# A graph attention kernel: one-hots split around the weights, gathers in two passes, keys in halves, and integer keys

## The chip, the cores and the metric

One core of a Trainium2 chip runs the whole kernel. The metric is the time of one execution on the device in microseconds (us). The profile is of one execution; its span, from first to last instruction, is some 2 us shorter than the time measured from outside, so I compare spans with spans and times with times. For one core, a run counts as fast when it is within 1.5% of the fastest of its kernel.

## The reference

```python
# x [4096, 64], edge_index [2, 50000], weight [4, 64, 64], att_src/att_dst [4, 64]
for h in range(4):
    x_proj[h] = x @ weight[h]
    edge_scores[h] = (x_proj[h, src] * att_src[h]).sum(-1) + (x_proj[h, dst] * att_dst[h]).sum(-1)
edge_scores = np.where(edge_scores > 0, edge_scores, 0.2 * edge_scores)
# output[h, dst] += exp(score) * x_proj[h, src], over all edges
# output[h, dst] /= (sum of exp(score) over the edges of dst) + 1e-8
return output.transpose(1, 0, 2).reshape(4096, 256)
```

## The kernel before

The 50,000 edges are sorted on VectorE in two passes, through memory, into 33 blocks of 125 destination nodes. Each block has 16 groups (one for each segment of 256 source nodes) of 128 edge slots. A window of sorted keys is unpacked into two small indices per slot (`tb`), written to a table in memory (`gat_bins`), and each block loads its piece of it, repeated over all partitions (`bc`). Block 0 does not go through memory: TensorE spreads `tb` over the partitions (`spread`).

In the loop, one-hot matrices (`oh`, an equality against the partition number) let TensorE gather each edge's features and attention terms into PSUM (`ps`). ScalarE takes the exponentials (`ex`) and copies the gathered rows (`xs`); VectorE makes the weights (`wv`, the larger of two exponentials) and the weighted features (`val`). Matmuls sum them per destination (`acc`), ScalarE copies the sums (`aT`), TensorE projects them (`pf`), and each second block VectorE divides (`inv`, `res`) and stores two blocks.

```python
class Windows:                                   # hand-over: keys -> indices
    def unpack(self, i, *engs):
        V.tensor_scalar(out=self.kb[:, i, :], in0=self.win[:, i, :], scalar1=boff[:, i:i + 1], scalar2=None, op0=OP.add)
        V.tensor_scalar(out=self.t[:, i, 0, :], in0=self.kb[:, i, :], scalar1=8, ..., op0=OP.logical_shift_right)
        V.tensor_scalar(out=self.t[:, i, 1, :], in0=self.kb[:, i, :], scalar1=SG - 1, ..., op0=OP.bitwise_and)
        V.tensor_copy(out=self.tb[:, i], in_=self.t[:, i])
        for k, eng in enumerate(engs):
            eng.dma_start(out=<bin_dram piece k of group i>, in_=self.tb[:, i, k, :])

CH = ((0, 6), (6, 6), (12, 4))                   # the 16 segments in three chunks
class Blocks:
    def gather(self, b, c, copy=S.copy):
        ...                                      # ps: two buffers
        for i in range(n):
            T.matmul(out=ps[:, i, P:P + XC], lhsT=oh[:, 1, e], rhs=xa[:, 2 * t, :], ...)
            T.matmul(out=ps[:, i, P:P + XC], lhsT=oh[:, 2, e], rhs=xa[:, 2 * t + 1, :], ...)
            T.matmul(out=ps[:, i, 0:S0], lhsT=oh[:, 0, e], rhs=adb[:, b, :], ...)
        S.activation(out=<ex>, in_=<ps>, func=ACTF.Exp)
        copy(out=xs[:, t0:t0 + n, 0:P + XC], in_=ps[:, 0:n, 0:P + XC])

    def run(self, also={}):
        for c in range(len(CH)):
            self.gather(0, c, V.tensor_copy if c == 1 else S.copy)
        self.onehot(1)                           # both halves: oh[:, 0:2], then oh[:, 2]
        for b in range(ND):
            self.load(b + 4)
            self.weigh(b, ...)                   # wv = max(ex0, ex1); val = xs * wv
            self.gather(b + 1, 0)
            self.onehot(b + 2)
            if b:
                self.sink.project(b - 1)
                if b % 2 == 0:
                    self.sink.give(b - 2, 2)     # inv, res, output
            self.sums(b, -1)                     # opens with a matmul on a vector of ones
            self.gather(b + 1, 1)
            self.gather(b + 1, 2)
            self.sums(b, 0)                      # the value matmuls
            self.sums(b, 1)
        ...

class Finish:                                    # pf: one buffer, of two blocks
    def project(self, b):
        for k in range(2):
            T.matmul(out=self.pf[0:BD, b % 2, k * P:(k + 1) * P], lhsT=self.aT[:, b % 2, k * BD:(k + 1) * BD], rhs=Wbd[:, k, :], ...)   # fp32, BD = 125
    def give(self, b, n):
        V.reciprocal(out=inv[0:BD, 0:n], ...)
        V.tensor_tensor(out=res[0:BD, 0:n], in0=<pf>, in1=<inv>, op=OP.mult)
        ...
```

## Time and profile before

| | before |
|---|---|
| time, median of 4 runs beside the changed kernel | 302.66 us (301.87 to 302.71) |
| span of the profiled run, mean granted clock | 300.1 us, 0.854 |
| busy: VectorE, PE, weight loads, ScalarE | 88%, 68%, 64%, 60% of the span |
| first operation of the first / second sort | 7.64 / 76.68 us |
| window of sorted keys in place | 120.14 us |
| first `val` | 133.29 us |
| `val` of block 3 to `val` of block 31 | 135.81 us |
| last `res` | 293.51 us |

The shares are averages over stages with different limits. The rows of times are what to read: keys and two sorts (VectorE alone), a hand-over between the window's arrival and the first `val`, and a steady loop of 33 blocks. The stretches and timelines that carry this are shown in the prediction.

### The profile page before, as it was taken

How to read it: one execution, taken by the hardware profiler on the slowest of the kernel's cores; microseconds unless marked ns; L12 is line 12 of the kernel's file. 1: busy time of each engine (PE TensorE's matmuls, PEld its weight loads, DVE VectorE, ACT ScalarE, POOL GpSimd, SP SyncE). 2: the span in 40 equal slices, each digit the busy share in tenths (PEclk: the TensorE clock that was granted, in tenths of full speed). 3: DMA queues.
4: the chain of work that ended last, by engine and by line, in shares of the span. 5: the costliest groups of instructions: out<-in, count | busy, mean ns of one | idle time of the engine just before them, and what ended most of it. 6: DMA issues, size and time to landing. Idle time of an engine off the chain costs nothing. (4 is left out here: it accounts for less than half of the span.)

```text
span 300.1 us, 8417 instructions
## 1 busy us (share of the span) xinstructions
PE 203.3 (68%) x3534; PEld 191.8 (64%) x3534; DVE 265.2 (88%) x493; ACT 180.4 (60%) x353; POOL 27.6 (9%) x77
## 2 busy tenths in 40 slices
PE   0001899950000003759999999999999999999980
PEld 0000599950000000449999999999999999999980
DVE  4999999994799995799999999999999999999970
ACT  2950710050699910347887778778777878787740
POOL 7982000002000002300000000000000000000000
PEclk9999975555555555798999999999999999999998
DMA  3025000001000001497486667865686667755012
GB/s 107 0 55 105 0 2 0 0 0 54 19 0 0 0 0 44 149 356 269 157 303 249 201 221 288 279 224 193 259 303 224 210 227 306 273 177 210 11 38 58
DMA packets 13070, 41.80 MB, mean 139 GB/s; under 512 B 3088, under 2 KB 8272, under 8 KB 8928
## 3 DMA queue, kind: packets, MB, share of 16 engines
q1 hardware_dynamic: 10632, 38.97, 36.5%
q10 hardware_dynamic: 1688, 1.55, 2.1%
q0 software_dynamic: 704, 0.66, 1.0%
q8 instruction: 30, 0.49, 0.7%
q14 instruction: 16, 0.13, 0.1%
HBM read 36.13 MB, written 5.05 MB: 137 GB/s over the span
## 5 line engine op out<-in xcount | busy, mean ns | idle before, releaser
L467 ACT CAST xs<-ps 128x1200 bf16<-128x1200 f32 (+1 forms) x98 | 102.7, 1048 | 0.0
L480 DVE TENSOR_TENSOR val<-xs,wv 128x4096 bf16<-128x4096 bf16 (+1 forms) x34 | 75.7, 2229 | 4.8 <-ACT xs L467 1.3
L459 PE MATMUL ps<-xa,oh 128*128 128x72 bf16 x528 | 72.3, 197 | 3.6 <-DVE oh L441 2.9
L463 PE MATMUL ps<-adb,oh 128*128 128x136 bf16 x528 | 73.2, 226 | 0.0
L461 PE MATMUL ps<-xa,oh 128*128 128x72 bf16 x528 | 71.5, 198 | 0.6 <-DVE oh L442 0.5
L499 PE MATMUL acc<-xs,val 128*128 128x125 bf16 x1056 | 64.0, 219 | 1.1
L499 PEld LDWEIGHTS <-val 128*128 128x128 bf16 x1056 | 59.4, 98 | 3.4 <-DVE val L480 3.4
L459 PEld LDWEIGHTS <-oh 128*128 128x128 bf16 x528 | 52.3, 99 | 3.5 <-DVE oh L441 3.5
L461 PEld LDWEIGHTS <-oh 128*128 128x128 bf16 x528 | 52.0, 99 | 2.0 <-DVE oh L442 1.4
L463 PEld LDWEIGHTS <-oh 128*128 128x128 bf16 x528 | 52.1, 99 | 0.0
L441 DVE TENSOR_SCALAR oh<-bc,pF 128x4096 bf16<-128x4096 bf16 (+2 forms) x35 | 42.7, 1220 | 0.6 <-ACT bc L425 0.6
L465 ACT ACTIVATE ex<-ps 128x96 bf16<-128x96 f32 (+1 forms) x99 | 25.1, 253 | 29.8 <-PE ps L463 29.8
L204 DVE TENSOR_TENSOR sA<-sB 128x256 f32<-128x256 f32 (+2 forms) x108 | 38.8, 400 | 1.9
L204 DVE TENSOR_TENSOR sB<-sA 128x256 f32<-128x256 f32 (+2 forms) x100 | 35.9, 400 | 1.7
L277 PE MATMUL cnt_ps<-sgn,sel 128*128 128x17 f32 (+1 forms) x6 | 1.7, 390 | 41.9 <-ACT sgn L269 41.9
L277 PEld LDWEIGHTS cnt_ps<-sgn,sel 128*128 128x128 f32 x6 | 1.4, 318 | 42.0 <-issue 42.0
L442 DVE TENSOR_SCALAR oh<-bc,pF 128x2048 bf16<-128x2048 bf16 (+2 forms) x35 | 25.1, 717 | 0.0
L361 PEld LDWEIGHTS at_ps<-uv,xT 64*128 64x128 f32 x130 | 24.7, 296 | 0.4 <-issue 0.4
L361 PE MATMUL at_ps<-uv,xT 64*128 64x4 f32 x130 | 24.8, 327 | 0.0
L266 ACT ACTIVATE junk<-kr,nb 128x512 f32<-128x512 f32 x33 | 23.8, 722 | 1.1
L545 PE MATMUL pf<-Wbd,aT 128*125 128x128 f32 x132 | 21.9, 288 | 0.9 <-ACT aT L541 0.9
L344 PE MATMUL ps<-ident,wS 64*128 64x64 f32 x2 | 0.7, 350 | 28.6 <-DMA wS<-in_weight_dram 28.6
(128 smaller groups left out, 222.5 us busy)
## 6 DMA issues: line engine op xcount, KB each, us to landing
bc<-gat_bins SPq DMA_DIRECT2D x32, 1024.0 KB, 8.9
out_dram<-res SPq DMA_DIRECT2D x32, 125.0 KB
gat_sorted<-sA SPq DMA_DIRECT2D x2, 256.0 KB
eS<-in_edge_index_dram SPq DMA_DIRECT2D x1, 390.0 KB
eD<-in_edge_index_dram ACTq DMA_DIRECT2D x1, 390.0 KB
gat_bins<-tb SPq DMA_DIRECT2D x9, 32.0 KB
out_dram<-res SPq DMA_DIRECT2D x1, 96.0 KB
win<-gat_sorted,wi POOLq DMA_INDIRECT x5, 2.7
```

Source lines behind the costliest of these rows:

```text
L204: V.tensor_tensor(out=av(d[:], o, [2 * h, n], [1, h]), in0=av(s[:], 0, [2 * h, n], [1, h]), in1=av(s[:], h, [2 * h, n], [1, h]), op=op)
L266: S.activation(out=junk[:], in_=v, func=ACTF.Sign, bias=nbnd[:, b:b + 1], scale=1.0, accum_out=sgn[:, b:b + 1])
L361: T.matmul(out=ps[:, b, :], lhsT=xT[:, b * step:b * step + P], rhs=uv[:, k, :], start=(b == 0), stop=True, skip_group_check=True)
L441: V.tensor_scalar(out=oh[:, 0:2, e], in0=bc[:, :, e], scalar1=pF[:, 0:1], scalar2=None, op0=OP.is_equal)
L442: V.tensor_scalar(out=oh[:, 2, e], in0=bc[:, 1, e], scalar1=pF[:, 1:2], scalar2=None, op0=OP.is_equal)
L459: T.matmul(out=ps[:, i, P:P + XC], lhsT=oh[:, 1, e], rhs=xa[:, 2 * t, :], start=(i % 2 == 0), stop=False, skip_group_check=True)
L461: T.matmul(out=ps[:, i, P:P + XC], lhsT=oh[:, 2, e], rhs=xa[:, 2 * t + 1, :], start=False, stop=False, skip_group_check=True)
L463: T.matmul(out=ps[:, i, 0:S0], lhsT=oh[:, 0, e], rhs=adb[:, b, :], start=False, stop=True, skip_group_check=True)
L465: S.activation(out=av(ex[:], 2 * t0, [2, n], [2 * NT, 2 * H], [1, 2]), in_=av(ps[:], P, [PW, n], [1, 2 * H], [0, 2]), func=ACTF.Exp)
L467: copy(out=xs[:, t0:t0 + n, 0:P + XC], in_=ps[:, 0:n, 0:P + XC])
L480: V.tensor_tensor(out=av(val[:], h * Dout, [Dout, n], [C, NT], [1, Din]), in0=av(xs[:], S0, [0, n], [XW, NT], [1, Din]), in1=av(wv[:], h * ...
L499: T.matmul(out=self.acc[:, k * BD:(k + 1) * BD], lhsT=val[:, t, k * P:(k + 1) * P], rhs=xs[:, t, 0:BD], start=False, stop=(t == NT - 1), s ...
```

## The change

Its intent: keep VectorE from waiting on its own previous result, and start each stage sooner. (1) In the loop `wv` of the next block moves between the two one-hot operations, and `inv` ahead of them, so that no operation directly follows the one whose result it reads. (2) The gather takes the matmuls that need the second one-hot half in a second pass. (3) The projection uses 128 weight columns. (4) In the hand-over: six warming matmuls for nine, a ScalarE copy in place of a VectorE one for block 0, shorter unpacking. (5) Input and first keys come in two halves. (6) The second sort's last step writes integers, which the unpacking then needs no conversion for.

```diff
+    EH = EL // 2
+    for e in (slice(0, EH), slice(EH, E0)):             # one load per tensor before
+        for t, k, eng in ((eS, 0, nc.sync), (eD, 1, nc.scalar)):
+            eng.dma_start(out=t[:, e, :], ...)
...
-        store(skey2, so.runs())
+        ki = pool.tile([P, L], I32, name="ki")
+        store(skey2, so.runs(ki))                       # skey2 is int32 now
...
         def unpack(self, i, *engs):
-            V.tensor_scalar(out=self.kb[:, i, :], in0=self.win[:, i, :], scalar1=boff[:, i:i + 1], ..., op0=OP.add)
-            ... shift, and, then V.tensor_copy(out=self.tb[:, i], in_=self.t[:, i])
+            t, tb = self.t[:, i], self.tb[:, i]
+            V.tensor_scalar(out=t[:, 1, :], in0=self.win[:, i, :], scalar1=SG - 1, ..., op0=OP.bitwise_and)
+            V.tensor_scalar(out=t[:, 0, :], in0=self.win[:, i, :], scalar1=8, ..., op0=OP.logical_shift_right)
+            (S.copy if i == 0 else V.tensor_copy)(out=tb[:, 1, :], in_=t[:, 1, :])
+            V.tensor_scalar(out=tb[:, 0, :], in0=t[:, 0, :], scalar1=boff[:, i:i + 1], ..., op0=OP.add)
...
                 T.matmul(out=ps[:, i, P:P + XC], lhsT=oh[:, 1, e], rhs=xa[:, 2 * t, :], ...)
-                T.matmul(out=ps[:, i, P:P + XC], lhsT=oh[:, 2, e], rhs=xa[:, 2 * t + 1, :], ...)
                 T.matmul(out=ps[:, i, 0:S0], lhsT=oh[:, 0, e], rhs=adb[:, b, :], ...)
+            for i in range(n):
+                T.matmul(out=ps[:, i, P:P + XC], lhsT=oh[:, 2, <e of i>], rhs=xa[:, 2 * t + 1, :], ...)
...
             for c in range(len(CH)):
-                self.gather(0, c, V.tensor_copy if c == 1 else S.copy)
+                self.gather(0, c)                       # ScalarE copies all three
             self.onehot(1)
+            self.weights(0)
             for b in range(ND):
                 self.load(b + 4)
-                self.weigh(b, ...)
+                self.values(b, ...)                     # val alone
                 self.gather(b + 1, 0)
-                self.onehot(b + 2)
                 if b:
                     self.sink.project(b - 1)
-                    if b % 2 == 0:
-                        self.sink.give(b - 2, 2)
                 self.sums(b, -1)
                 self.gather(b + 1, 1)
                 self.gather(b + 1, 2)
+                pair = b and b % 2 == 0
+                if pair:
+                    self.sink.invert(2)
+                self.onehot(b + 2, halves=(0,))
+                self.weights(b + 1)
+                self.onehot(b + 2, halves=(1,))
+                if pair:
+                    self.sink.give(b - 2, 2)            # res, output
                 self.sums(b, 0)
                 self.sums(b, 1)
...
-                T.matmul(out=self.pf[0:BD, b % 2, ...], lhsT=self.aT[:, b % 2, k * BD:(k + 1) * BD], ...)
+                T.matmul(out=self.pf[:, b % 2, ...], lhsT=self.aT[:, b % 2, k * BD:k * BD + P], ...)
...
+        for e, n in ((0, EH), (EH, EL - EH)):           # the four key operations, on one half at a time
...
-        for i in range(9):
+        for i in range(6):
             T.matmul(out=warm[:], lhsT=identb[:], rhs=adb[:, 0:4, 0:P], start=True, stop=True)
```

More of the change, by code (lines that the diff above doesn't have):

```diff
@@ L59 @@
     skey1 = nc.dram_tensor("gat_sorted1", (1, P * L + W1), F32).ap()
-    skey2 = nc.dram_tensor("gat_sorted2", (1, P * L + W2), F32).ap()
+    skey2 = nc.dram_tensor("gat_sorted2", (1, P * L + W2), I32).ap()
     bin_dram = nc.dram_tensor("gat_bins", (8 * NI, 2, NR, W2), BF16).ap()
@@ L70 @@
     eD = cst.tile([P, EL, 2], I32)
-    for t, k, eng in ((eS, 0, nc.sync), (eD, 1, nc.scalar)):
-        eng.dma_start(out=t[:, 0:E0, :], in_=ei[k, 0:P * E0, :].rearrange("(p e) c -> p e c", p=P))
+    EH = EL // 2
+    for e in (slice(0, EH), slice(EH, E0)):
+        for t, k, eng in ((eS, 0, nc.sync), (eD, 1, nc.scalar)):
+            eng.dma_start(out=t[:, e, :], in_=ei[k, 0:P * E0, :].rearrange("(p e) c -> p e c", p=P)[:, e, :])
     if rem:
@@ L141 @@
     pg = cst.tile([P, 1], F32)
-    G.tensor_scalar(out=pg[:], in0=pm16[:], scalar1=-float(SG * N), scalar2=None, op0=OP.mult)
+    G.tensor_scalar(out=pg[:], in0=pm16[:], scalar1=-float(N), scalar2=None, op0=OP.mult)
     for i in range(NI):
-        G.tensor_scalar(out=boff[:, i:i + 1], in0=p16[:], scalar1=-float(BD * SG), scalar2=-float(8 * i * BD * SG),
+        G.tensor_scalar(out=boff[:, i:i + 1], in0=p16[:], scalar1=-float(BD), scalar2=-float(8 * i * BD),
                         op0=OP.mult, op1=OP.add)
@@ L161 @@
     nc.gpsimd.dma_start(out=skey1[0:1, P * L:P * L + W1], in_=pad[:])
-    nc.gpsimd.dma_start(out=skey2[0:1, P * L:P * L + W2], in_=pad[:, 0:W2])
+    padi = cst.tile([1, W2], I32)
+    G.tensor_copy(out=padi[:], in_=pad[:, 0:W2])
+    nc.gpsimd.dma_start(out=skey2[0:1, P * L:P * L + W2], in_=padi[:])
     identb = cst.tile([P, P], BF16)
@@ L197, in flip, with half @@
                             in1=av(s[:], h - 1, [2 * h, n], [-1, h]), op=OP.max)
-        def half(self, j, width=L):
+        def half(self, j, width=L, to=None):
             s, d = self.step()
+            d = to or d
             h = 1 << j
@@ L233, in turn, with runs @@
             V.transpose(out=d[:], in_=s[:])
-        def runs(self):
+        def runs(self, to=None):
             s, d = self.step()
@@ L253, in runs @@
                 for j in range(8, -1, -1):
-                    self.half(j)
-            return self.a[self.cur]
+                    self.half(j, to=to if m == 2 and j == 0 else None)
+            return to or self.a[self.cur]
     def store(skey, t):
@@ L374, in __init__ @@
         def __init__(self, pool, start):
-            self.win = pool.tile([P, NI, W2], F32, name="win")
-            self.kb = pool.tile([P, NI, W2], I32, name="kb")
+            self.win = pool.tile([P, NI, W2], I32, name="win")
             self.t = pool.tile([P, NI, 2, W2], I32, name="t")
@@ L381, in unpack @@
         def unpack(self, i, *engs):
-            V.tensor_scalar(out=self.kb[:, i, :], in0=self.win[:, i, :], scalar1=boff[:, i:i + 1], scalar2=None,
-                            op0=OP.add)
-            V.tensor_scalar(out=self.t[:, i, 0, :], in0=self.kb[:, i, :], scalar1=8, scalar2=None,
+            t, tb = self.t[:, i], self.tb[:, i]
+            V.tensor_scalar(out=t[:, 1, :], in0=self.win[:, i, :], scalar1=SG - 1, scalar2=None, op0=OP.bitwise_and)
+            V.tensor_scalar(out=t[:, 0, :], in0=self.win[:, i, :], scalar1=8, scalar2=None,
                             op0=OP.logical_shift_right)
-            V.tensor_scalar(out=self.t[:, i, 1, :], in0=self.kb[:, i, :], scalar1=SG - 1, scalar2=None,
-                            op0=OP.bitwise_and)
-            V.tensor_copy(out=self.tb[:, i], in_=self.t[:, i])
+            (S.copy if i == 0 else V.tensor_copy)(out=tb[:, 1, :], in_=t[:, 1, :])
+            V.tensor_scalar(out=tb[:, 0, :], in0=t[:, 0, :], scalar1=boff[:, i:i + 1], scalar2=None, op0=OP.add)
             for k, eng in enumerate(engs):
@@ L417, in spread @@
         def spread(self, b, tb):
-            bc = self.bcp.tile([P, 2, NT * W2], BF16, name="bc")
+            bc = self.bc[b] = self.bcp.tile([P, 2, NT * W2], BF16, name="bc")
             for c, (t0, n) in enumerate(CH):
@@ L427, in spread, with onehot, gather @@
                 if c == 1:
-                    self.onehot(b, bc, *CH[0])
+                    self.onehot(b, *CH[0])
             for c in (1, 2):
-                self.onehot(b, bc, *CH[c])
-        def onehot(self, b, bc=None, t0=0, nt=NT):
-            if b < ND:
-                if bc is None:
-                    bc = self.bc.pop(b)
-                if t0 == 0:
-                    self.oh[b] = self.bp.tile([P, 3, NT * W2], BF16, name="oh")
-                oh = self.oh[b]
-                e = slice(t0 * W2, (t0 + nt) * W2)
-                V.tensor_scalar(out=oh[:, 0:2, e], in0=bc[:, :, e], scalar1=pF[:, 0:1], scalar2=None, op0=OP.is_equal)
-                V.tensor_scalar(out=oh[:, 2, e], in0=bc[:, 1, e], scalar1=pF[:, 1:2], scalar2=None, op0=OP.is_equal)
-        def gather(self, b, c, copy=S.copy):
+                self.onehot(b, *CH[c])
+        def onehot(self, b, t0=0, nt=NT, halves=(0, 1)):
+            if b >= ND:
+                return
+            if t0 == 0 and halves[0] == 0:
+                self.oh[b] = self.bp.tile([P, 3, NT * W2], BF16, name="oh")
+            oh, bc = self.oh[b], self.bc[b]
+            e = slice(t0 * W2, (t0 + nt) * W2)
+            for i in halves:
+                if i == 0:
+                    V.tensor_scalar(out=oh[:, 0:2, e], in0=bc[:, :, e], scalar1=pF[:, 0:1], scalar2=None,
+                                    op0=OP.is_equal)
+                else:
+                    V.tensor_scalar(out=oh[:, 2, e], in0=bc[:, 1, e], scalar1=pF[:, 1:2], scalar2=None,
+                                    op0=OP.is_equal)
+        def gather(self, b, c):
             if b >= ND:
@@ L460, in gather, with weights @@
                          skip_group_check=True)
-                T.matmul(out=ps[:, i, P:P + XC], lhsT=oh[:, 2, e], rhs=xa[:, 2 * t + 1, :], start=False, stop=False,
+                T.matmul(out=ps[:, i, 0:S0], lhsT=oh[:, 0, e], rhs=adb[:, b, :], start=False, stop=False,
                          skip_group_check=True)
-                T.matmul(out=ps[:, i, 0:S0], lhsT=oh[:, 0, e], rhs=adb[:, b, :], start=False, stop=True,
-                         skip_group_check=True)
+            for i in range(n):
+                t = t0 + i
+                T.matmul(out=ps[:, i, P:P + XC], lhsT=oh[:, 2, t * W2:(t + 1) * W2], rhs=xa[:, 2 * t + 1, :],
+                         start=False, stop=True, skip_group_check=True)
             S.activation(out=av(ex[:], 2 * t0, [2, n], [2 * NT, 2 * H], [1, 2]),
                          in_=av(ps[:], P, [PW, n], [1, 2 * H], [0, 2]), func=ACTF.Exp)
-            copy(out=xs[:, t0:t0 + n, 0:P + XC], in_=ps[:, 0:n, 0:P + XC])
+            S.copy(out=xs[:, t0:t0 + n, 0:P + XC], in_=ps[:, 0:n, 0:P + XC])
             if c == len(CH) - 1:
-                self.oh.pop(b)
-        def weigh(self, b, parts=1):
-            xs, ex = self.xs[b], self.ex.pop(b)
+                self.oh.pop(b), self.bc.pop(b)
+        def weights(self, b):
+            if b >= ND:
+                return
+            ex = self.ex.pop(b)
             wv = self.bp.tile([P, H, NT, 2], BF16, name="wv")
@@ L476, in weigh, with values @@
             self.wv[b] = wv
+        def values(self, b, parts=1):
+            xs, wv = self.xs[b], self.wv[b]
             val = self.bp.tile([P, NT, C], BF16, name="val")
@@ L506, in run @@
             for c in range(len(CH)):
-                self.gather(0, c, V.tensor_copy if c == 1 else S.copy)
+                self.gather(0, c)
             self.onehot(1)
+            self.weights(0)
             for b in range(ND):
                 self.load(b + 4)
-                self.weigh(b, 2 if b == ND - 1 else 1)
+                self.values(b, 2 if b == ND - 1 else 1)
                 self.gather(b + 1, 0)
-                self.onehot(b + 2)
                 if b:
                     self.sink.project(b - 1)
-                    if b % 2 == 0:
-                        self.sink.give(b - 2, 2)
                 self.sums(b, -1)
@@ L526, in run @@
             n = 2 - ND % 2
+            self.sink.invert(n)
             self.sink.give(ND - n, n)
@@ L544, in project, with invert @@
             for k in range(2):
-                T.matmul(out=self.pf[0:BD, b % 2, k * P:(k + 1) * P], lhsT=self.aT[:, b % 2, k * BD:(k + 1) * BD],
+                T.matmul(out=self.pf[:, b % 2, k * P:(k + 1) * P], lhsT=self.aT[:, b % 2, k * BD:k * BD + P],
                          rhs=Wbd[:, k, :], start=(b % 2 == 0 and k == 0), stop=True, skip_group_check=True)
+        def invert(self, n):
+            self.inv = self.fp.tile([P, 2, H], F32, name="inv")
+            V.reciprocal(out=self.inv[0:BD, 0:n], in_=self.aT[0:BD, 0:n, 2 * BD:AW])
         def give(self, b, n):
-            inv = self.fp.tile([P, 2, H], F32, name="inv")
-            V.reciprocal(out=inv[0:BD, 0:n], in_=self.aT[0:BD, 0:n, 2 * BD:AW])
             res = self.fp.tile([P, 2, H, Dout], F32, name="res")
             V.tensor_tensor(out=res[0:BD, 0:n], in0=av(self.pf[0:BD], 0, [Dout, n * H], [1, Dout]),
-                            in1=av(inv[0:BD], 0, [1, n * H], [0, Dout]), op=OP.mult)
+                            in1=av(self.inv[0:BD], 0, [1, n * H], [0, Dout]), op=OP.mult)
             for i in range(n):
@@ L569, in project, with invert @@
         def project(self, b):
+            pass
+        def invert(self, n):
             pass
@@ L596 @@
             V.memset(t[:, EL:L], KPAD)
-        src = av(eS[:], 0, [2, EL])
-        dst = av(eD[:], 0, [2, EL])
-        sgn = below(so1, src, EL, nb1, NR, NR)
-        V.tensor_scalar(out=sli[:], in0=src, scalar1=SG - 1, scalar2=None, op0=OP.bitwise_and)
-        V.tensor_scalar(out=tF[:], in0=sli[:], scalar1=1.0 - N, scalar2=None, op0=OP.mult)
-        V.scalar_tensor_tensor(out=uF[:], in0=dst, scalar=float(SG), in1=tF[:], op0=OP.mult, op1=OP.add)
-        V.scalar_tensor_tensor(out=key[:, 0:EL], in0=src, scalar=float(N), in1=uF[:], op0=OP.mult, op1=OP.add)
+        sgn = below(so1, av(eS[:], 0, [2, EL]), EL, nb1, NR, NR)
+        for e, n in ((0, EH), (EH, EL - EH)):
+            src = av(eS[:], 2 * e, [2, n])
+            dst = av(eD[:], 2 * e, [2, n])
+            c = slice(e, e + n)
+            V.tensor_scalar(out=sli[:, c], in0=src, scalar1=SG - 1, scalar2=None, op0=OP.bitwise_and)
+            V.tensor_scalar(out=tF[:, c], in0=sli[:, c], scalar1=1.0 - N, scalar2=None, op0=OP.mult)
+            V.scalar_tensor_tensor(out=uF[:, c], in0=dst, scalar=float(SG), in1=tF[:, c], op0=OP.mult, op1=OP.add)
+            V.scalar_tensor_tensor(out=key[:, c], in0=src, scalar=float(N), in1=uF[:, c], op0=OP.mult, op1=OP.add)
         tables(pr, pps, pp1)
@@ L656 @@
                     if b % 2 or b == ND - 1:
+                        fin.invert(b % 2 + 1)
                         fin.give(b - b % 2, b % 2 + 1)
```

## The prediction

> **What bounds the kernel now.** I read the page first for its stages, then a table of busy time by stretches, then the three engines' timelines over a few blocks of the main loop, then the timeline of the hand-over from the second sort to the loop. The stages: keys and first sort to 69 us, fetch and second sort from 76 to 115 us, hand-over to about 133 us, then 33 blocks, tail from 289 us. Both sorts lie on VectorE alone and the change leaves their instructions as they are, so the loop (about half of the span) and the hand-over decide. The stretches of the loop (columns: stretch, its length, busy us of PE, PEld, DVE, ACT, POOL with counts, granted clock, DMA share, GB/s):
>
> ```profile
> 160.00:200.00 40.00, 39.61 (x834) 38.60 (x832) 38.69 (x42) 31.38 (x58) 0.00 (x0) 1.00 0.70 248
> 200.00:240.00 40.00, 39.69 (x833) 38.83 (x831) 38.69 (x42) 31.74 (x59) 0.00 (x0) 1.00 0.70 246
> 240.00:280.00 40.00, 39.69 (x836) 38.79 (x833) 38.56 (x43) 31.03 (x58) 0.00 (x0) 1.00 0.63 226
> ```
>
> TensorE and VectorE both look full, so shares cannot say which one sets the pace. The VectorE timeline can (columns: start us, us, engine, line, operation, operands):
>
> ```profile
> 143.55 2.29 DVE L480 TENSOR_TENSOR val<-xs,wv 128x4096 bf16<-128x4096 bf16 x1 [0.29 <-ACT xs L467]
> 145.76 1.28 DVE L441 TENSOR_SCALAR oh<-bc,pF 128x4096 bf16<-128x4096 bf16 x1
> 146.96 0.75 DVE L442 TENSOR_SCALAR oh<-bc,pF 128x2048 bf16<-128x2048 bf16 x1
> 147.62 0.20 DVE L550 RECIPROCAL inv<-aT 125x8 f32<-125x8 f32 x1
> 147.92 0.69 DVE L552 TENSOR_TENSOR res<-pf,inv 125x512 f32<-125x512 f32 x1
> 148.53 0.22 DVE L475 TENSOR_TENSOR wv<-ex 128x128 bf16<-128x128 bf16 x1
> 148.85 2.29 DVE L480 TENSOR_TENSOR val<-xs,wv 128x4096 bf16<-128x4096 bf16 x1
> 151.06 1.28 DVE L441 TENSOR_SCALAR oh<-bc,pF 128x4096 bf16<-128x4096 bf16 x1
> 152.25 0.75 DVE L442 TENSOR_SCALAR oh<-bc,pF 128x2048 bf16<-128x2048 bf16 x1
> 152.92 0.22 DVE L475 TENSOR_TENSOR wv<-ex 128x128 bf16<-128x128 bf16 x1
> 153.27 2.29 DVE L480 TENSOR_TENSOR val<-xs,wv 128x4096 bf16<-128x4096 bf16 x1
> ```
>
> Start to start, a block that gives output takes 5.30 us (143.55 to 148.85), the other 4.42 us; the pair repeats to the end (158.56, 162.98), 9.71 us, 4.85 a block. From 148.85 on VectorE never waits for another engine, so it sets the pace. TensorE's own pace is just below: where VectorE does not hold it, the matmul on the vector of ones that opens each block's sums comes every 4.68 us (144.66, 149.34 in the PE timeline); 149.34 to 158.98 is 9.64, the slack going into waits for val. So VectorE can give back at most 9.71 - 2 x 4.68 = 0.35 us a pair before TensorE binds: 5.2 us over the 15 pairs.
>
> The hand-over:
>
> ```profile
> 118.48 4.00 PE L616 MATMUL warm<-adb,identb 128*128 128x512 bf16 x9 [0.70 <-DVE most L296]
> ...
> 122.53 2.07 PE L423 MATMUL ps<-tb,identb 128*128 128x256 bf16 x12
> ...
> 124.11 2.78 ACT L425 CAST bc<-ps 128x1536 bf16<-128x1536 f32 x2 [18.10 <-DMA win<-gat_sorted,wi]
> ...
> 125.58 0.62 DVE L441 TENSOR_SCALAR oh<-bc,pF 128x1536 bf16<-128x1536 bf16 x1 [0.56 <-ACT bc L425]
> ...
> 129.78 1.41 DVE L467 CAST xs<-ps 128x1200 bf16<-128x1200 f32 x1 [0.61 <-ACT ex L465]
> ...
> 131.11 1.28 DVE L441 TENSOR_SCALAR oh<-bc,pF 128x4096 bf16<-128x4096 bf16 x1
> 132.30 0.75 DVE L442 TENSOR_SCALAR oh<-bc,pF 128x2048 bf16<-128x2048 bf16 x1
> 132.44 0.10 PEld L459 LDWEIGHTS <-oh 128*128 128x128 bf16 x1 [2.64 <-DVE oh L441]
> ```
>
> The index tile tb is ready at 121.18 us, but nine warming matmuls hold TensorE to 122.5. Then VectorE copies xs (1.41 us) before it makes the one-hots of block 1, and TensorE idles.
>
> **What the skill says.** "VectorE: DVE Perf Modes", The DRAIN you can't avoid: a Vector result read by the next Vector instruction needs a semaphore, or an instruction between. The trace agrees in size: wv to val takes 0.35 or 0.32 us start to start, inv to res 0.30, while two independent small operations (the two of the unpacking, 142.44 and 142.58) stand 0.14 apart with durations of 0.22 and 0.23. "TensorE: Matmul & The Clock Gate", Weight-path perf modes: the fast weight load needs 128 weight columns and a type other than FP32. The trace agrees: attention matmuls with 128 fp32 columns and 4 moving columns run 11 in one us at clock 1.00, some 91 ns each, against some 28 ns for bf16 weights with 4 columns (16 from 144.69 to 145.11). Same page, Part 1: an idle window lets the clock fall to half. It does: granted 0.52 at 134 us and 0.50 to 137 us, after the gap above.
>
> **The change part by part.**
> 1. *One-hots around the weights.* wv now stands between the two one-hot operations, and inv before them. val no longer follows wv: 0.35 becomes 0.14 (0.32 in the giving block), and inv to res 0.30 becomes 0.12 to an independent operation. Saved on VectorE: 0.21 + 0.18 + 0.18 = 0.57 us a pair, leaving 9.14, below TensorE's 9.36. But wv needs the last exp of the next block, and now comes 0.66 us earlier (1.5 in a giving block). Put O for the ones matmul. The last exp starts at O + 2.58 (161.56 - 158.98), ends 0.25 later, so wv may start at O + 2.87. The value matmuls start at O + 1.69 if val ended by O + 1.63, so val must start by O - 0.66. Let v be val's start against O. Plain block: wv at the later of v + 3.41 (2.21 + 1.20) and 2.87; next val 0.80 later. Giving block: wv at the later of v + 3.52 and 2.87; next val 1.41 later (0.14 + 0.66 + 0.61). From v = -1.00, giving: VectorE reaches wv at 2.52 and waits 0.35; next val at 4.28, -0.40 against the next O. Plain: wv 3.01, next val 3.81, TensorE is held 0.26, so this block takes 4.94 and v is -1.13. The pair repeats at 4.68 + 4.94 = 9.62. A second hold leads to the same place: res now ends at O + 4.42 with its semaphore, and the projection of the next block, which overwrites pf (one buffer), wants to start at O + 4.19. So most of the 0.57 turns into VectorE's wait for exp: I book 9.71 - 9.62 = 0.09 a pair, x 14 = 1.2 us.
> 2. *Gathers in two passes.* The same 48 matmuls and weight loads a block; 72 columns cost 30 ns start to start and 136 cost 60 in either order. Its worth is that the second half of the one-hots may come later; else TensorE would stand at the start of the gather. 0.
> 3. *128 instead of 125 columns in the projection.* fp32, no fast load by the above: 3 columns more in 4 passes, under 0.01 us. 0.
> 4. *Hand-over.* Six warming matmuls instead of nine at 427 ns: TensorE free 1.28 us sooner. Unpacking loses one of four serial steps (0.29 to 0.32 us) and its last cast, for the first group partly on ScalarE: tb at about 120.85. ScalarE's copy of bc starts about 1.4 us sooner, but the unpacking of the fourth group stands ahead of the one-hots on VectorE, and its data are there only by 124.0; plus 0.75 gives 124.75 instead of 125.58. The xs copy goes to ScalarE, off VectorE's path (1.41). Block 1's one-hots then wait for their transfer: shortest issue to landing 5.5 us, issued at about 124.4, hence 129.9 instead of 131.11. First val at about 132.0 instead of 133.29. Booked 1.3 us.
> 5. *Keys in two halves.* Before: data at 5.64, four operations to 7.64. Traffic ran from 1.5 to 4.9 us, so the first halves may land near 4.0 and the second near 5.8; four half operations take about 1.3 us: 7.1 to 7.5. Booked 0.4 us.
> 6. *Integers out of the second sort.* The same operation with another output type: 0; its gain is in part 4.
> Sum: 1.2 + 1.3 + 0.4 = 2.9 us.
>
> **The rivals.** (a) TensorE becomes the only bound, 4.68 a block, because exp comes earlier or the slack between blocks absorbs the hold: 0.35 x 15 = 5.2 us instead of 1.2, total near 295.7. For it: VectorE work of 9.14 fits. Against: an in-order VectorE behind an exp that ScalarE starts only at O + 2.58, after two 1.15 us copies. (b) Projection weights load fast at 128 columns: up to 0.15 us a block more, near 294. Against: 91 ns above. (c) VectorE waits longer for exp than the recurrence says, or smaller edge transfers are slower: gain near 0, 302. For it: ex is the most waited for tile of ScalarE (20.7 us in 160 to 285). (d) The gap at the start is short enough that the clock stays high: 1.5 us more, or the shift moves it only, which I expect.
>
> **Range and chances.** 302.6 less 2.9 is 299.7; (a) and (d) are likelier than (c), so I say 299.3. A range of 296.2 to 301.6 holds everything but (a) in full and (b). 2% is 296.6: faster 0.18, within 0.80, slower 0.02.
>
> **What would show it.** Right: val starts pairwise about 9.62 apart; a wait of 0.3 us of wv for ex in every second block; TensorE waiting for val or, at the projection, for res; wv to the next one-hot about 0.14; first val near 132; keys done near 7.2; projection passes unchanged. Wrong: a pair at 9.36 with no wait on wv (rival a), a block under 4.68 (b), a pair at or above 9.71 (c), block 1 waiting for its transfer beyond 131.

## The result

The changed kernel takes 300.06 us (median of 4 runs, 299.21 to 300.15) against 302.66 us, a ratio of 0.9914 with a 95% interval of 0.989 to 0.9938: a small gain, within 2%. A ratio here is the mean time of one kernel's fast runs over that of the other's in the same rounds, so it is not quite the ratio of the medians quoted.

| us | before | after | gained by then |
|---|---|---|---|
| first operation of the first sort | 7.64 | 7.02 | 0.62 |
| first operation of the second sort | 76.68 | 76.76 | -0.08 |
| window of sorted keys in place | 120.14 | 120.27 | -0.13 |
| block 1's indices: load issued | 124.71 | 123.46 | 1.25 |
| block 1's one-hots start | 131.11 | 128.92 | 2.19 |
| first `val` | 133.29 | 131.11 | 2.18 |
| `val` of block 3 | 148.85 | 146.25 | 2.60 |
| `val` of block 31 | 284.66 | 282.33 | 2.33 |
| last `res` | 293.51 | 291.33 | 2.18 |
| span | 300.1 | 298.1 | 2.0 |

So the whole gain arises between the window's arrival and the first values. The keys' 0.62 us are gone before the second sort starts, and the loop gives nothing: 135.81 us from block 3 to block 31 before, 136.08 after.

One stretch of the loop after, in the same columns as before (length; busy us of PE, weight loads, VectorE, ScalarE, POOL; clock, DMA share, GB/s):

```profile
200.00:240.00 40.00, 39.47 (x837) 38.97 (x837) 38.08 (x41) 31.67 (x58) 0.00 (x0) 1.00 0.69 246
```

VectorE is busy 0.6 us less in 40 (38.69 before) with the same work done: the dependent steps have become shorter, and the time freed is idle. Where it idles, VectorE's timeline shows (a bracket at the end of a line is the idle time before it and what ended it):

```profile
150.66 2.28 DVE L495 TENSOR_TENSOR val<-xs,wv 128x4096 bf16<-128x4096 bf16 x1
152.86 0.20 DVE L573 RECIPROCAL inv<-aT 125x8 f32<-125x8 f32 x1
152.97 1.24 DVE L446 TENSOR_SCALAR oh<-bc,pF 128x4096 bf16<-128x4096 bf16 x1
154.56 0.23 DVE L487 TENSOR_TENSOR wv<-ex 128x128 bf16<-128x128 bf16 x1 [0.36 <-ACT ex L475]
154.71 0.75 DVE L449 TENSOR_SCALAR oh<-bc,pF 128x2048 bf16<-128x2048 bf16 x1
155.37 0.68 DVE L577 TENSOR_TENSOR res<-pf,inv 125x512 f32<-125x512 f32 x1
155.97 2.28 DVE L495 TENSOR_TENSOR val<-xs,wv 128x4096 bf16<-128x4096 bf16 x1
...
159.57 0.23 DVE L487 TENSOR_TENSOR wv<-ex 128x128 bf16<-128x128 bf16 x1
...
160.38 2.28 DVE L495 TENSOR_TENSOR val<-xs,wv 128x4096 bf16<-128x4096 bf16 x1
```

The giving block takes 5.31 us from `val` to `val`, the plain one 4.41: 9.72 a pair against 9.71. The chain was broken up as intended (`wv` to the one-hot after it 0.15, `inv` to the one-hot 0.11, where dependent steps took 0.30 to 0.35), but in the giving block `wv` stands 0.36 us for `ex`. The list of waits between 160 and 285 us (waiter, what it waited for, us in total, times, longest) says how often:

```profile
ACT ex L475 <- PE ps L473: 24.2, 52, 0.7
DVE wv L487 <- ACT ex L475: 4.7, 13, 0.4
PEld pf L568 <- issue: 3.0, 13, 0.2
```

Both lower lines come 13 times in 125 us, once a pair. The third is TensorE's own stop, put down to "issue" because the profile saw no releaser. All engines together, around that stop, in the timeline after:

```profile
155.71 0.36 PE L473 MATMUL ps<-xa,oh 128*128 128x72 bf16 x6
...
156.17 0.52 PEld L568 LDWEIGHTS pf<-Wbd,aT 128*128 128x128 f32 x4 [0.23 <-issue]
156.20 0.68 PE L568 MATMUL pf<-Wbd,aT 128*128 128x128 f32 x4
```

The second pass of the gather starts at 155.71 and the projection 0.49 us later; in the plain block before it, it starts 0.19 us later (151.00 and 151.19). `res` ends at 156.05, and the projection, which overwrites the `pf` that `res` reads, begins 0.15 us after that. So TensorE is held 0.30 us in every second block, and its pair is 4.71 + 5.01 us between the ones matmuls: it now sets the pace.

In the kernel before, the list of waits for the same stretch has another line in that place:

```profile
PEld L499 <- DVE val L480: 3.0, 13, 0.2
```

There TensorE stood for `val` in every second block, the plain one, and its pair was 4.70 + 5.00 us. The change took this hold away (the value matmuls now start 1.68 or 1.69 us after the ones matmul in both kinds of block; 1.68 and 1.93 before) and put one of the same size in its place.

The hand-over after, from TensorE's, ScalarE's and VectorE's timelines:

```profile
118.55 2.72 PE L646 MATMUL warm<-adb,identb 128*128 128x512 bf16 x6 [0.69 <-DVE most L301]
121.34 2.50 PE L427 MATMUL ps<-tb,identb 128*128 128x256 bf16 x12
122.87 2.78 ACT L429 CAST bc<-ps 128x1536 bf16<-128x1536 f32 x2 [2.04 <-DMA gat_bins<-tb]
124.62 0.61 DVE L446 TENSOR_SCALAR oh<-bc,pF 128x1536 bf16<-128x1536 bf16 x1
128.92 1.29 DVE L446 TENSOR_SCALAR oh<-bc,pF 128x4096 bf16<-128x4096 bf16 x1 [0.71 <-DMA bc<-gat_bins]
131.11 2.29 DVE L495 TENSOR_TENSOR val<-xs,wv 128x4096 bf16<-128x4096 bf16 x1
```

The `xs` copy is gone from VectorE, and block 1's one-hots now wait for their indices. Half of the table is stored, and these loads are issued, on the sync engine's queue, in the kernel before

```profile
121.21 0.74 SPq L390 DMA_DIRECT2D gat_bins<-tb  x1
124.71 1.24 SPq L413 DMA_DIRECT2D bc<-gat_bins  x3
```

and in the changed kernel

```profile
121.22 0.73 SPq L394 DMA_DIRECT2D gat_bins<-tb  x1
123.46 1.28 SPq L417 DMA_DIRECT2D bc<-gat_bins  x3
```

The loads are issued 4.57 and 3.19 us after the window's arrival. The store ahead of them leaves 1.07 and 0.95 us after it, only 0.12 sooner: most of the gain, 1.26 us, lies between store and load, 3.50 and 2.24 us. The drop of TensorE's clock in this gap remained: granted 0.52 and 0.50 from 134 to 137 us before, 0.65, 0.50 and 0.65 from 130 to 134 after.

Last, the keys. VectorE before the second sort, in the kernel before:

```profile
71.45 0.17 DVE L307 CAST wi<-ws 128x2 int32<-128x2 f32 x1
76.68 0.43 DVE L194 TENSOR_TENSOR sA<-raw 128x256 f32<-128x256 f32 x1 [5.06 <-DMA raw<-gat_sorted,wi]
```

and in the changed kernel:

```profile
68.83 0.17 DVE L287 TENSOR_TENSOR pick<-cnt,m 128x16 f32<-128x16 f32 x1 [0.46 <-DVE cnt L284]
71.50 0.17 DVE L312 CAST wi<-ws 128x2 int32<-128x2 f32 x1 [0.43 <-issue]
76.76 0.42 DVE L198 TENSOR_TENSOR sA<-raw 128x256 f32<-128x256 f32 x1 [5.09 <-DMA raw<-gat_sorted,wi]
```

The first sort's store was issued 0.63 us sooner (68.31 against 68.94), but two stops, at `pick` and at `wi`, that the kernel before does not have use it up before the window starts `wi` are known, and these start the fetch.

### The profile page after: what moved, and what is told of

The parts are those of the page before. It is cut to its first block, busy times and chain, and to the rows that moved or that the text cites. A ratio compares the mean times of both kernels' runs of the same rounds, so it can differ in the third digit from the quotient of the medians.

```text
span 298.1 us, 8429 instructions
## 1 busy us (share of the span) xinstructions
PE 201.9 (68%) x3531; PEld 192.3 (64%) x3531; DVE 261.6 (88%) x495; ACT 181.7 (61%) x355; POOL 27.3 (9%) x78
## 4 chain that ended last, share of the span: by engine, by line
PE 53%; DVE 35%; DMA 5%; issue 3%; POOL 1%; ACT 0%; DVEq 0%; SPq 0%; POOLq 0%
PE acc L514 20%; DVE sA L209 13%; DVE sB L209 12%; PE ps L469 10%; PE pf L568 7%; PE ps L467 6%; PE ps L473 6%; PE acc L509 5%; DMA bc<-gat_bins 2%; DVE sB L238 1%; DMA eS<-in_edge_index_dram 1%; DMA raw<-gat_sorted,wi 1%; DVE sA L198 1%; DMA win<-gat_sorted,wi 1%; DMA gat_bins<-tb 1%
## 5 line engine op out<-in xcount | busy, mean ns | idle before, releaser
L477 ACT CAST xs<-ps 128x1200 bf16<-128x1200 f32 (+1 forms) x99 | 104.1, 1051 | 0.0
L469 PE MATMUL ps<-adb,oh 128*128 128x136 bf16 x528 | 62.5, 225 | 0.0
L467 PE MATMUL ps<-xa,oh 128*128 128x72 bf16 x528 | 59.7, 198 | 3.0 <-DVE oh L446 2.2
L514 PEld LDWEIGHTS <-val 128*128 128x128 bf16 x1056 | 58.8, 98 | 0.2 <-DVE val L495 0.2
L469 PEld LDWEIGHTS <-oh 128*128 128x128 bf16 x528 | 49.7, 99 | 0.3 <-issue 0.3
L467 PEld LDWEIGHTS <-oh 128*128 128x128 bf16 x528 | 47.4, 99 | 3.1 <-DVE oh L446 3.1
L446 DVE TENSOR_SCALAR oh<-bc,pF 128x4096 bf16<-128x4096 bf16 (+2 forms) x35 | 42.0, 1201 | 0.7 <-DMA bc<-gat_bins 0.7
L209 DVE TENSOR_TENSOR sA<-sB 128x256 f32<-128x256 f32 (+2 forms) x106 | 38.0, 400 | 1.8
L473 PE MATMUL ps<-xa,oh 128*128 128x72 bf16 x528 | 33.7, 199 | 0.0
L473 PEld LDWEIGHTS <-oh 128*128 128x128 bf16 x528 | 26.7, 100 | 0.0
L568 PE MATMUL pf<-Wbd,aT 128*128 128x128 f32 x132 | 22.7, 295 | 2.9 <-ACT aT L564 0.9
L568 PEld LDWEIGHTS pf<-Wbd,aT 128*128 128x128 f32 x132 | 17.3, 191 | 4.7 <-issue 3.4
```

Source lines behind the costliest of these rows:

```text
L209: V.tensor_tensor(out=av(d[:], o, [2 * h, n], [1, h]), in0=av(s[:], 0, [2 * h, n], [1, h]), in1=av(s[:], h, [2 * h, n], [1, h]), op=op)
L446: V.tensor_scalar(out=oh[:, 0:2, e], in0=bc[:, :, e], scalar1=pF[:, 0:1], scalar2=None, op0=OP.is_equal)
L473: T.matmul(out=ps[:, i, P:P + XC], lhsT=oh[:, 2, t * W2:(t + 1) * W2], rhs=xa[:, 2 * t + 1, :], start=False, stop=True, skip_group_check=True)
L477: S.copy(out=xs[:, t0:t0 + n, 0:P + XC], in_=ps[:, 0:n, 0:P + XC])
L514: T.matmul(out=self.acc[:, k * BD:(k + 1) * BD], lhsT=val[:, t, k * P:(k + 1) * P], rhs=xs[:, t, 0:BD], start=False, stop=(t == NT - 1), s ...
L568: T.matmul(out=self.pf[:, b % 2, k * P:(k + 1) * P], lhsT=self.aT[:, b % 2, k * BD:k * BD + P], rhs=Wbd[:, k, :], start=(b % 2 == 0 and k ...
```

## The experiments

Theory: the loop gains nothing because `res` is late and holds the projection (and VectorE waits for `ex`), and the gain of 2.6 us is the hand-over's. Rivals: TensorE itself became slower (two passes, 128 columns), so that no order of VectorE could help; and the earlier keys or the warming matmuls brought the gain. Each kernel below is an edit of the changed kernel unless it says otherwise, and all gave correct results. Its time stands beside the kernel before of the same rounds, 302.58 to 302.65 us.

### Where the loop's gain went

**a1_res_early**: `res` before `wv` and the second one-hot half.

```diff
                 self.onehot(b + 2, halves=(0,))
+                if pair:
+                    self.sink.give(b - 2, 2)
                 self.weights(b + 1)
                 self.onehot(b + 2, halves=(1,))
-                if pair:
-                    self.sink.give(b - 2, 2)
```

> The changed kernel with one move: the multiplication that makes res and frees pf stands before the weights, not behind the second one-hot half. Theory 1, the held projection: in every giving block wv waits 0.36 us for the last exp, res comes behind it and ends at O + 4.34, so the next block's projection, which overwrites the single pf buffer, starts at O + 4.49 instead of O + 4.19. With res ahead of wv it ends near O + 3.3, the hold of 0.30 us goes, and a pair of blocks takes 2 x 4.71 = 9.42 instead of 9.72: 4.3 us over 14 to 15 pairs, total near 295.8. Rival, the exp wait: VectorE stays late because it waits for exp, val holds the sums instead, the pair stays at 9.65 to 9.72, total 299.5 to 300.

Measured: 296.74 us (296.04 to 299.91, 6 runs), ratio 0.9837 (0.9802 to 0.9872); span 294.1. The waits from 150 to 280 us:

```profile
ACT ex L475 <- PE ps L473: 21.6, 55, 0.4
DVE wv L487 <- ACT ex L475: 3.9, 14, 0.3
```

and VectorE in a giving block:

```profile
163.52 0.68 DVE L577 TENSOR_TENSOR res<-pf,inv 125x512 f32<-125x512 f32 x1
164.12 0.21 DVE L487 TENSOR_TENSOR wv<-ex 128x128 bf16<-128x128 bf16 x1
```

The line of `pf` is gone from the waits, every block takes TensorE 4.71 us, and the pair 9.42. In the giving block `wv` comes after `res` and waits no more; the 14 waits of 0.28 us that remain are the plain blocks', and cost nothing, since TensorE is not held for `val`. One place in VectorE's order was worth 0.30 us a pair: 4.0 us of the span, 3.3 of the median. By the ratios (0.9837 against 0.9914) it is some 2.3 us; the intervals do not overlap. This shows that the hold on the projection ate the loop's gain, and that TensorE's own pace did not forbid it. The slowest of the six runs had the lowest mean clock (0.834, the others 0.848 to 0.853), so not all of the spread is the kernel's.

**a2_proj125**: the projection back at 125 columns, nothing else.

```diff
-   out=self.pf[:, b % 2, ...],    lhsT=self.aT[:, b % 2, k * BD:k * BD + P]
+   out=self.pf[0:BD, b % 2, ...], lhsT=self.aT[:, b % 2, k * BD:(k + 1) * BD]
```

> The changed kernel with the projection's weights at 125 columns again, as in the kernel before. The traces say that 128 columns made the four passes 0.03 us longer (projection to the ones matmul 0.52 instead of 0.49): a block 0.03 us shorter, a pair 9.66, 0.9 us over the kernel, total near 299.2. Rival, that the wider load was a gain hidden by the hold on pf: the pair stays at 9.72 or rises, total 300 or more.

Measured: 299.07 us (298.81 to 301.51, 6 runs), ratio 0.991 (0.9882 to 0.9938). The pair is 9.70 (4.70 + 5.00) and the hold on the projection stays, 3.0 us in 13 times. The columns cost 0.01 us a block, less than the 0.03 that I had given them here.

**a3_both**: a1 and a2 together.

> Both of these moves together: res before the weights and 125 columns. Theory 1 expects TensorE alone to set the pace, 4.68 us for each block and 9.36 for a pair, no wait of the projection or of the value matmuls: total near 294.9, some 2.5 per cent under the kernel before. Rival, the exp wait: 299 or more.

Measured: 296.13 us (294.45 to 297.88, 5 runs), ratio 0.9809 (0.9784 to 0.9833); blocks of 4.70 to 4.71 us, pair 9.41. I had hoped for the 4.68 of the kernel before; the rest, 0.02 to 0.03 us a block, is then not the columns'. It lies between the projection's start and the next ones matmul: 0.51 to 0.52 us here, 0.48 to 0.49 in c1 below, which differs by the one pass alone, while the gathers themselves take as long in the kernel before. This kernel has the lowest median, 1.9% under the kernel before by the mean of its runs and 1.3% under the changed one by the medians; its interval overlaps that of a1, and whether it is 2% faster than the kernel before is unclear.

**c1_onepass**: a3 with the three matmuls of a segment together again.

```diff
                 T.matmul(out=ps[:, i, P:P + XC], lhsT=oh[:, 1, e], ...)
+                T.matmul(out=ps[:, i, P:P + XC], lhsT=oh[:, 2, e], ...)
                 T.matmul(out=ps[:, i, 0:S0], lhsT=oh[:, 0, e], ...)
-            for i in range(n):
-                T.matmul(out=ps[:, i, P:P + XC], lhsT=oh[:, 2, <e of i>], ...)
```

> The fast version (res ahead of the weights, 125 columns) with the gathers in one pass again, as in the kernel before; the one-hots stay split around the weights. The second one-hot half now follows wv, which cannot start before the last exp, at O + 2.86: it ends at O + 3.75, while the next gather could start at O + 3.46 and needs it in its second matmul. If the two passes are what makes the split order possible, the gather is held about 0.3 us in every block, a block takes about 5.02 us instead of 4.70, and the total rises by some 10 us to 306. If the passes do not matter: 296.1, or a little less, as the passes seem to cost 0.02 us a block.

Measured: 305.24 us (304.24 to 305.45, 4 runs), ratio 1.0094 (1.0061 to 1.0127); blocks of 5.00 us. The waits from 150 to 280 us have two lines new to this loop:

```profile
PEld L469 <- DVE oh L449: 7.9, 26, 0.3
PE ps L469 <- DVE oh L449: 4.1, 26, 0.2
```

Line 469 here is the matmul on the second half of the one-hots, in every block: with `wv` between the halves, this half comes too late for a gather in one pass. Two passes bring nothing by themselves, but without them the new order of VectorE costs 0.3 us a block, and would have made the kernel slower than before.

**a4_oldloop**: VectorE's order of the kernel before, all other parts of the change kept.

```diff
+                self.weights(b)
                 self.values(b, ...)
                 self.gather(b + 1, 0)
+                self.onehot(b + 2)
                 if b:
                     self.sink.project(b - 1)
+                    if b % 2 == 0:
+                        self.sink.invert(2)
+                        self.sink.give(b - 2, 2)
...                                              # and these calls taken out further down
```

> The changed kernel with the loop's VectorE order of the kernel before (weights right before values, both one-hot halves together, reciprocal and result behind them); hand-over, keys, integers, two passes and 128 columns as in the changed kernel. If the whole gain comes from the hand-over, this is as fast as the changed kernel within 0.4 us, 299.6 to 300.2, with a pair at 9.71. If the new order earns the 1.2 us that the prediction booked, it is near 301.3.

Measured: 300.3 us (299.77 to 300.84, 6 runs), ratio 0.9931 (0.9914 to 0.9948); pair 9.71 (4.75 + 4.96; two pairs of this profile took 0.35 more), first `val` at 130.89. Nearly the whole gain is there without the new order.

**b1_looponly**: the kernel before with the new loop (order, two passes, 128 columns) alone; keys, unpacking, warming matmuls and the first `xs` copy as before.

> The kernel before with the loop part of the change alone: one-hots around the weights, reciprocal early, gathers in two passes, 128 columns; keys, float keys, unpacking, nine warming matmuls and the copy of xs on VectorE as before. The traces say that the loop part is worth nothing (a pair 9.72 instead of 9.70): 302.4 to 303.2, first val at about 133.3. If the new order earns 1.2 us as booked: 301.4.

Measured: 302.2 us (301.57 to 303.22, 4 runs), ratio 0.9994 (0.9964 to 1.0024); pair 9.72. Together with a4 this settles that the loop's part was worth nothing as it was written, in the loop. (Its first `val` came 12.59 us after the window, 0.56 sooner than before; see b4.)

### Where the hand-over's gain came from

**b4_xsv**: the middle `xs` copy of block 0 back on VectorE.

```diff
-                self.gather(0, c)
+                self.gather(0, c, V.tensor_copy if c == 1 else S.copy)
```

> The changed kernel with the middle copy of xs of block 0 on VectorE, as before. It waits for the gather of that chunk (exp of it starts at 128.24), so it runs from about 128.5 to 129.9 and the one-hots of block 1 start at about 129.9 instead of 128.92: first val 0.9 to 1.0 us later, 301.0. If the transfer sets the start anyway: no change, 300.1.

Measured: 300.73 us (300.64 to 300.82, 4 runs), ratio 0.9941 (0.9924 to 0.9958). VectorE's timeline:

```profile
128.28 1.41 DVE L477 CAST xs<-ps 128x1200 bf16<-128x1200 f32 x1 [0.31 <-ACT ex L475]
129.60 1.28 DVE L446 TENSOR_SCALAR oh<-bc,pF 128x4096 bf16<-128x4096 bf16 x1
```

Here the copy, not the indices, is what block 1's one-hots wait for. The first `val` came at 131.78, 11.84 us after this run's window (119.94), against 10.84 in the changed kernel and 13.15 before. So of the 2.31 us the copy, taken out last, is 1.00 in the profile (0.67 in the medians of the times), and 1.31 are left. Of these, 1.00 is that block 0's one-hots start 4.44 us after the window instead of 5.44, and 0.30 that the copy waits 0.31 us for `ex` instead of 0.61. This shorter wait is in b1 too (0.31), so it comes with the new loop code, not with the hand-over's own edits. The shares depend on the order: the copy was not taken out of the kernel before alone.

**b3_warm9**: nine warming matmuls again.

```diff
-        for i in range(6):
+        for i in range(9):
```

> The changed kernel with nine warming matmuls instead of six. The spread of block 0 then starts 1.28 us later (122.6 instead of 121.34), ScalarE copies bc at about 124.2, the one-hots of block 0 start at about 125.6 instead of 124.62 and end at about 129.2; those of block 1 had 0.71 us of slack against their transfer (128.92), so the first val comes 0.2 to 0.4 us later: 300.3 to 300.5. If the warming matmuls were the main part of the hand-over's gain (1.3 us or more): 301.4.

Measured: 299.84 us (299.47 to 300.23, 4 runs), ratio 0.9913 (0.9893 to 0.9933); first `val` 10.93 us after the window (130.99 and 120.06). A miss: the one-hots of block 0 come at 125.19 instead of 124.62, but block 1's at 128.79, when their indices are there. The warming matmuls lie on the path of block 0, and this path no longer ends last. In the changed kernel they contribute nothing; with the copy still on VectorE, where block 0's path ends last, they were not tried.

**b5_castv**: the one cast that went to ScalarE (block group 0) on VectorE.

```diff
-            (S.copy if i == 0 else V.tensor_copy)(out=tb[:, 1, :], in_=t[:, 1, :])
+            V.tensor_copy(out=tb[:, 1, :], in_=t[:, 1, :])
```

> The changed kernel with the first group's cast of the node index on VectorE instead of ScalarE. In the changed kernel the load of block 1's indices is issued 3.1 to 3.25 us after the first window lands, in the kernels with the old unpacking 4.3 to 4.6 us. If the gain comes from ScalarE's own cast, which lets its half of the table leave 0.36 us ahead of the other: the load comes at about 3.5 or later and the first val 0.3 us or more later, 300.4. If it comes from the shorter chain alone: within 0.15 us, 300.1.

Measured: 299.83 us (299.19 to 301.48, 5 runs), ratio 0.9913 (0.9885 to 0.9942). The first half of the table was stored 0.53 us after the window, as in the changed kernel (0.59; 1.08 before), and block 1's load issued 3.31 us after it (3.19; 4.57 before). So the earlier issue is not the ScalarE cast's doing. Nor is it the shorter chain of steps alone, for the later of the two stores leaves only 0.12 us sooner in the changed kernel (0.95 us after the window, 1.07 before). From that store to the load it took 3.50, 3.26 and 3.40 us in the three profiles with the old unpacking (before, b1, d1) and 2.16 to 2.54 in the ten with the new one, so this part of the gain goes with the new unpacking and its integer keys (loop, halves, warming matmuls, copy and cast were each taken back among the ten). In the old one the two stores were issued within 0.01 us of each other, in the new one 0.12 to 0.42 us apart. Whether this is why the load could follow sooner, no run tries; this stays open.

### The keys

**b2_keyswhole**: the changed kernel with whole inputs and whole keys.

```diff
-    EH = EL // 2
-    for e in (slice(0, EH), slice(EH, E0)):
+    EH = EL
+    for e in (slice(0, E0),):
...
-        for e, n in ((0, EH), (EH, EL - EH)):
+        for e, n in ((0, EL),):
```

> The changed kernel with the keys in one piece. In the changed kernel the keys were done 0.62 us earlier, but VectorE then stood twice (0.46 us ahead of the first pick, 0.43 us ahead of the window starts) and the second sort began 0.08 us later than in the kernel before. If those stops take the place of the gain whatever the keys do (something else is late there), this kernel starts the second sort at 76.6 to 76.8 too and takes the same time within 0.2 us, 300.1. If the stops come from the instruction stream of the changed kernel itself, they stay and it starts the second sort at about 77.4, 0.6 us slower, 300.7.

Measured: 299.69 us (299.13 to 300.47, 4 runs), ratio 0.9917 (0.989 to 0.9943). The keys are done at 7.56 and the second sort starts at 76.91, only 0.15 later than in the changed kernel (76.76), because the stop at `pick` is absent; the one at `wi` is there, 0.43. Without the halves the kernel is as fast.

**d1_keysonly**: the kernel before with the two halves alone.

> The kernel before with the keys in two halves and nothing else. The keys should be done at about 7.0 us instead of 7.64. If the two stops of VectorE ahead of the second sort (0.35 us more than usual each) come with the halves, as in all the kernels with them so far, the second sort starts at 76.6 to 76.8 and the time is that of the kernel before within 0.2 us, 302.6. If the stops come from other parts of the change, it starts at about 76.0 and the total is 302.0.

Measured: 301.6 us (301.3 to 302.29, 4 runs), ratio 0.999 (0.9961 to 1.002). The median is 1.0 us under that of the kernel before, the ratio of the means within the rounds only 0.1%, with 1 inside the interval: the time does not show a difference. In the profile the keys are done at 6.71, `pick` stops for 0.46, `wi` does not stop, and the second sort starts at 75.94, 0.74 us sooner than before; the first `val` comes 0.74 sooner as well (132.55). So a gain in the keys can reach the second sort. One stop goes with the halves, the other with some other part of the change (it is in every kernel that has the rest of the change, with halves or without, and not in the kernel before, b1 or d1). Why VectorE stops there I do not know: the profile names an operation long done, or "issue". This stays open.

## Why the prediction was right, and where it was not

The time on record, 299.3 us, was 0.8 us low, and the range and the class held. Of its sum of 2.9 us the measured counterpart is 2.6, but the parts are not those that were booked: loop and keys were booked 1.6 us too high, the hand-over 0.9 to 1.0 too low. That the total came so near was luck.

1. *The loop: booked 1.2, measured 0.* The mechanisms were named rightly. `wv` waits in the giving block (0.35 foreseen, 0.36 measured), and `res` meets the projection's overwrite of `pf`. What failed is the size of two terms of the pair, "4.68 + 4.94 = 9.62". The hold, 0.26 in it, came out at 0.30: of the two holds the prediction took the second to lead "to the same place" as the first, with `res` releasing the projection at O + 4.42, where it ended at O + 4.34 and released it at O + 4.49. The first hold did not occur at all: the value matmuls start at O + 1.68 or 1.69 in both kinds of block, since the projection's hold puts O itself later and `val` after a giving block starts at O - 0.75, not at O - 0.40. And TensorE's own block is 4.71, not 4.68. The pair is 2 x 4.71 + 0.30 = 9.72, 0.10 us above the 9.62: 0.06 from the two blocks and 0.04 from the hold, and together enough to undo the gain of 0.09. The prediction should have worked its second hold out to the end.
2. *Two passes: booked 0.* Nearly right in cost (0.02 to 0.03 us a block, a3 beside c1), and right in purpose: c1 shows the stop that they avoid.
3. *128 columns: right*, 0.01 us a block, no fast load (rival b did not occur).
4. *Hand-over: booked 1.3, measured 2.2 by the clock of the span, 2.3 from the window.* The copy's removal was one step (1.00). The indices of block 1 were the next wait, as foreseen, but the issue was put at 124.4 and the landing at 129.9; they were 123.46 and 128.92. The term that failed is "issued at about 124.4": it gave the load 0.3 us where it came 1.25 sooner. The forecast of `tb` at 120.85 was wrong as well (complete at 121.20, 121.18 before), so the gain is not the unpacking's length; it lies between store and load. Warming matmuls and the ScalarE cast, which the prediction counted on the way, contributed nothing to the changed kernel (b3, b5).
5. *Keys: booked 0.4, measured 0.* The step itself was undersized (0.62), but the two stops took it back. Nothing in the profile before pointed at them.
6. *Integers: right*, the sort's last step kept its duration.

Two readings need a correction that changes no sum. The 16 small bf16 matmuls from 144.69 to 145.11 are 26 ns each, not 28. And the 20.7 us at `ex`, used for rival (c), are ScalarE waiting for TensorE, not VectorE waiting for `ex`.

Rival (a), TensorE as the only bound, was argued against with the exponential's lateness. The runs show that this argument held for the changed kernel only because of the hold on `pf`: with `res` early (a1, a3), the exponential waits remain and the pair is nearly (a)'s 9.36. Rival (c) described the loop (a pair at or above 9.71), but not the total. Rival (d)'s expectation, that the clock's drop only moves, held in these two profiles: by quarters of a us it lasted from 134.0 to 137.4 before and from 130.3 to 133.7 after, some 3.4 us both times. Its place and length vary from run to run: with the same hand-over b5's profile has 0.50 from 130 to 136 us (6.8 us in all), and a3's no drop from 128 to 140. The varying place and the lengths of 3.4 and 6.8 us agree with the Trainium skill, "TensorE: Matmul & The Clock Gate", Part 1, which calls the activity window of 3413 ns free-running. For this reason milestones behind 131 us carry about 1 us of uncertainty: block 0 to block 1 took 5.34 us in one profile and 6.84 in another.

## What to carry to other kernels

When two in-order engines are within a few per cent of each other, removing stalls on one only counts if its outputs for the other also come sooner: write down for each result that the neighbour reads, or each buffer that it will overwrite, when it comes before and after a reordering, and put the one that is awaited first. Here `res`, which frees a single-buffered tile, belonged ahead of `wv`, and moving that one call was worth about as much as the whole change (2.3 to 3.3 us beside 2.6). And a step that starts later work, like a load issued from an earlier store, is to be sized from its own chain of issue and landing, not from the engine whose time was freed.

## What the Trainium skill lacked or had wrong

- "VectorE: DVE Perf Modes", The DRAIN you can't avoid, says that a dependent step needs a semaphore or an instruction between, and that an operation not held starts earlier. Its one timing of this, eight copies with and without semaphores, shows no difference; it gives no cost for a small dependent step. The runs show 0.30 to 0.35 us start to start for small dependent operations and 0.11 to 0.15 for a small operation followed by an independent one.
- "Perfetto Trace Analysis", Per-engine timelines, shows the propagation of a semaphore outside the recorded window and gives no length. In these traces `ex` on ScalarE to `wv` on VectorE took 0.03 us from end to start, and `res` on VectorE to the projection on TensorE 0.15 us (0.12 to its weight load). Part of the hold that the prediction sized too small lies here.
- No page that I found accounts for VectorE's stops of about 0.35 us more than usual, at `pick` and at `wi`, that came and went with unrelated parts of the change.
